# A stick-breaking attention trunk on one core: one transposed block in four split by ScalarE and GpSimd, and the running product's ones kept in a PSUM bank

## The chip, the core and the metric

The kernel runs on one core of a Trainium2 chip. A core has a matrix engine (TensorE, PE in the tables, with its weight loads as PEld), three engines that work element by element on 128 partitions (VectorE or DVE, ScalarE or ACT, GpSimd or POOL), a queue engine (SyncE, SP), a large on-chip memory (SBUF) and a small accumulator memory (PSUM) of 8 banks, each 128 x 512 float32. Each engine works through its own list of instructions in a fixed order, and waits on semaphores for what other engines and transfers have to deliver. The metric is the device time of one execution in microseconds (us); lower is better.

## The reference

A trunk of two layers on x of 2048 positions and 1024 channels, in float32. Layer 0 is a gated short convolution. Layer 1 is attention of 8 heads of width 64 without a softmax: a score z gives the weight exp(z + sum of log sigmoid(-z) over the keys from this one to the query), which is a difference of two neighbours of a running product of sigmoid(-z). The kernel therefore multiplies the running product itself with differences of neighbouring rows of v, and adds the first row.

```
z = jnp.einsum("bhqd,bhkd->bhqk", qb, kf[:, :, :kl]) * scale
mask = jnp.arange(kl)[None, :] < q_pos[:, None]
log_one_minus = jnp.where(mask, jax.nn.log_sigmoid(-z), 0.0)
rev = lax.cumsum(log_one_minus, axis=3, reverse=True)
weights = jnp.exp(jnp.where(mask, z + rev, -jnp.inf))
outs.append(jnp.einsum("bhqk,bhkd->bhqd", weights, vf[:, :, :kl]))
```

Around it stand RMS norms, one projection each for k and v and for q and the gate, `(o * silu(g)) @ w_out_b`, a residual and a last norm.

## The kernel before

The positions are reversed, so that the running product goes forward, and cut into four chunks of 512. Every float32 matmul is done as three matmuls in a reduced float format: an operand x is split in a high part (ScalarE copies it, with rounding) and a low part (x minus the high part, VectorE). That is `split` (L486), and its two instructions stand in the profile as CAST and TENSOR_TENSOR.

The attention (`attention`, L1050) goes over heads h, query chunks c and key chunks kc from c down to 0; one (c, h, kc) is a unit. Where kc equals c the unit is on the diagonal; 48 units of 80 lie off it (8 heads times 1 + 2 + 3). In a unit:

- for each of four query blocks qi: the scores z are two matmuls into a PSUM tile of tag "z" (L1073), of which there are NZ = 3; ScalarE takes sigmoid(-z/8) out of it into R in SBUF, which frees the bank; VectorE makes the running product of R in place (`tensor_tensor_scan`, L1083), with a column of `ones` (L390, in SBUF, read over and over) as its second operand and the last element of the key chunk before as its start; GpSimd copies R's last column to `cy`, the start of the next key chunk; on the diagonal GpSimd also fills above the diagonal (AFFINE_SELECT).
- for each of four key blocks kb from 3 down to 0: TensorE transposes the four R blocks into a PSUM tile `wt` (two of them), `split` (L1102) takes it out as `wth` and `wtl` in SBUF, and two matmuls with v add to `av`, the one PSUM tile of the head's output.

PSUM has its 8 banks given out in full: 2 for "lin" (projections), 3 for "z", 2 for "wt", 1 for "av". Banks of "z" also serve other stages (L615, L833, and the last products at L1202).

The order of the work is not written out. Every operation is recorded first; `places` gives each a place from PLAN, a table of two numbers for each part (an attention head of a chunk is "a" and two digits); and `order` runs a model of the engines in which the earliest operation that can start is taken, ties going by place, with costs from `cost` and buffers counted. `emit` (L351) then writes the instructions in that order, so nearly all have the line L353 in the profile, and each engine keeps its order whatever happens. In the model, VectorE and GpSimd take turns (`o.turns`, L220) where an instruction has two operands in SBUF and none in PSUM. The attention heads are mixed with projections (pk, pq, pv, pg), with the output projection of finished chunks (pob) and with the last norm of those (x2r). Transfers are issued from SyncE's and ScalarE's queues; those of k, v and q for the attention are ScalarE's.

Of the kernel before, what the change touches and what calls it, by code (L numbers as in the profile page):

```python
# [10 lines left out]
F32 = mybir.dt.float32  # L11
# [5 lines left out]
P = 128  # L17
# [4 lines left out]
CH = 512  # L22
# [3 lines left out]
Q, NPL = 4, 2  # L26
FIRST = (("act", [2, CH], NA), ("R", [CH], NR), ("q2", [2, CH], 2), ("kt", [CH], 2), ("vv", [CH], 2), ("wth", [CH], NWTS),
         ("wtl", [CH], NWTS), ("wraw", [Q, P], NRAW), ("whl", [2, Q, P], NWB))
NLIN, NZ, NWT, NAV = 2, 3, 2, 1

XNL = (0, 3, 6)
YLP = (2, 5)
# [329 lines left out]
def kernel(  # L362
# [15 lines left out]
    nc = Recorder(tc.nc)  # L378

    const = Pool(nc, "const", ctx.enter_context(tc.tile_pool(name="const", bufs=1)))  # L380
    psum = Pool(nc, "psum", ctx.enter_context(tc.tile_pool(name="psum", bufs=2, space=bass.MemoryType.PSUM)))
    dram = Pool(nc, "dram", ctx.enter_context(tc.tile_pool(name="dram", bufs=1, space=bass.MemoryType.DRAM)))
    sb = Pool(nc, "sb", ctx.enter_context(tc.tile_pool(name="sb", bufs=2)))
# [5 lines left out]
    make_identity(tc.nc, ident.real())  # L389
    ones = const.tile([P, P], F32, name="ones")  # L390
    nc.vector.memset(ones, 1.0)
    gains = {}

    def load_gain(name, src, eng=nc.gpsimd):
# [91 lines left out]
    def split(hi, lo, src, eng=nc.vector):  # L486
        nc.scalar.copy(hi, src)
        eng.tensor_sub(lo, src, hi.bitcast(F32))
# [561 lines left out]
    def attention(c, h, ot):  # L1050

        hb, hi_ = divmod(h, 2)
        nm0 = f"{c}_{h}"
        q2 = sb.tile([P, 2, CH], F32R, name=f"q2_{nm0}", tag="q2", bufs=2)
        for i in range(2):
            nc.scalar.dma_start(out=q2[i * 64:(i + 1) * 64, :, :].bitcast(F32), in_=q_d[c][hb][hi_ * 64:(hi_ + 1) * 64, :, :])
        av = psum.tile([P, CH], F32, name=f"av_{nm0}", tag="av", bufs=NAV)
        carry = [None] * 4
        for kc in range(c, -1, -1):
            nm = f"{nm0}_{kc}"  # L1060
            diag = kc == c
            own = (h + kc) % 2 == 0
            kt = sb.tile([P, CH], F32R, name=f"kt_{nm}", tag="kt" if own else "wraw", bufs=2 if own else NRAW)
            nc.scalar.dma_start(out=kt.bitcast(F32), in_=k_d[kc][h])
            vt = sb.tile([P, 4, 2, 64], F32R, name=f"vv_{nm}", tag="vv" if own else "wraw", bufs=2 if own else NRAW)
            nc.scalar.dma_start(out=vt.bitcast(F32), in_=v_d[kc][hb][:, hi_, :, :, :])
            ws = []
            if kc:
                cy = sb.tile([P, 4], F32, name=f"cy_{nm}", tag="cy", bufs=8)
            for qi in range(4):  # L1070
                lo = qi * P if diag else 0
                lom = min(lo, 256)
                ps = psum.tile([P, CH], F32, name=f"z_{nm}_{qi}", tag="z", bufs=NZ)  # L1073
                nc.tensor.matmul(ps[:, lom:CH], q2[:, 0, qi * P:(qi + 1) * P], kt[:, lom:CH], start=True, stop=False)
                nc.tensor.matmul(ps[:, lom:CH], q2[:, 1, qi * P:(qi + 1) * P], kt[:, lom:CH], start=False, stop=True)
                R = sb.tile([P, CH], F32, name=f"R_{nm}_{qi}", tag="R", bufs=NR)
                nc.scalar.activation(R[:, lo:CH], ps[:, lo:CH], AF.Sigmoid, scale=-0.125)
                if diag:

                    blk = R[:, lo:lo + P]  # L1080
                    nc.gpsimd.affine_select(out=blk, in_=blk, pattern=[[1, P]], base=0, channel_multiplier=-1,
                                            compare_op=ALU.is_gt, fill=1.0)
                nc.vector.tensor_tensor_scan(out=R[:, lo:CH], data0=R[:, lo:CH],  # L1083
                                             data1=ones[:, 0:1].to_broadcast([P, CH - lo]),
                                             initial=1.0 if diag else carry[qi], op0=ALU.mult, op1=ALU.mult)
                if kc:
                    nc.gpsimd.tensor_copy(cy[:, qi:qi + 1], R[:, CH - 1:CH])
                    carry[qi] = cy[:, qi:qi + 1]
                ws.append(R)
            for kb in range(3, -1, -1):  # L1090
                nq = kb + 1 if diag else 4
                n = max(256, nq * P)
                wt = psum.tile([P, CH], F32, name=f"wt_{nm}_{kb}", tag="wt", bufs=NWT)
                for qi in range(nq):
                    nc.tensor.transpose(wt[:, qi * P:(qi + 1) * P], ws[qi][:, kb * P:(kb + 1) * P], ident)
                first, final = diag and kb == 3, kc == 0 and kb == 0
                wh = sb.tile([P, CH], F32R, name=f"wth_{nm}_{kb}", tag="wth", bufs=NWTS)
                wl = sb.tile([P, CH], F32R, name=f"wtl_{nm}_{kb}", tag="wtl", bufs=NWTS)
                if nq == 1:
                    nc.gpsimd.memset(wh[:, P:2 * P].bitcast(F32), 0.0)  # L1100
                    nc.gpsimd.memset(wl[:, P:2 * P].bitcast(F32), 0.0)
                split(wh[:, 0:nq * P], wl[:, 0:nq * P], wt[:, 0:nq * P])  # L1102
                vs = vt[:, kb, :, :].rearrange("p a d -> p (a d)")
                nc.tensor.matmul(av[:, 0:n], vs, wh[:, 0:n], start=first, stop=False)
                nc.tensor.matmul(av[:, 0:n], vs, wl[:, 0:n], start=False, stop=final)
            if kc == 0:
                osl = slice(hi_ * 64, hi_ * 64 + 64)
                oth = slice(64 - hi_ * 64, 128 - hi_ * 64)
                nc.scalar.copy(ot[osl, :], av[oth, :])
                nc.vector.tensor_add(ot[osl, :], ot[osl, :], av[osl, :])  # L1110
# [154 lines left out]
    for c in range(NCH):  # L1265
        for hb in range(NH // 2):
            ot = sb.tile([P, CH], F32, name=f"ot_{c}_{hb}", tag="ot", bufs=2)
            for h in (2 * hb, 2 * hb + 1):
                part(f"a{c}{h}", attention, c, h, ot)
            if (c, hb) == (3, 3):  # L1270
                last_ot.append(ot)
            else:
                nc.sync.dma_start(out=og_d[c][hb], in_=ot)
# [37 lines left out]
```

## Time and profile before

| | |
|---|---|
| three executions | 1681.12, 1681.06, 1673.86 us, median 1681.06 |
| the profiled execution | 1683.09 us, its span 1680.9 us |
| share of the span in work: TensorE, VectorE, ScalarE, GpSimd | 97%, 80%, 47%, 31% |
| granted TensorE clock, mean | 0.992 |
| running products of 512 elements with a start from `cy` | 192, 1311 ns each |
| low parts of 512 elements from `wt` | 224, 680 ns each |

The span is what the profile shows from its first instruction to its last; 2.2 us of the profiled execution lie outside it. Times in a row of a group are the busy time of the whole group, then the mean of one instruction, then the engine's idle time just ahead of them and what ended it. A matmul's row is its latency, longer than the step to the next one, since matmuls are pipelined.

### The profile page before, as it was taken

Reading aid. Unit: us, or ns where it says so; the run is one execution under the profiler, and the core shown is the slowest. Engines: PE = TensorE matmul, PEld = TensorE weight load, DVE = VectorE, ACT = ScalarE, POOL = GpSimd, SP = SyncE. Lnnn points to the kernel's source line nnn. Section 1 sums busy time; section 2 is a strip of 40 time slices with the busy share of each in tenths; the row PEclk is TensorE's granted clock in tenths of the full one; section 3 lists DMA queues with packets and bytes.
Section 4 is the critical chain, followed back from the end, with each engine's and each line's share of the span. In section 5 each row is a group of like instructions: output and inputs, shape, how many; then the busy total and the mean of one; then the engine's idle time right before and its main releaser. Section 6 shows DMA issues by size and latency. Waiting matters only on the chain.

```text
span 1680.9 us, 23871 instructions
## 1 busy us (share of the span) xinstructions
PE 1623.6 (97%) x7828; PEld 1339.8 (80%) x7828; DVE 1345.1 (80%) x1944; ACT 787.7 (47%) x1483; POOL 524.6 (31%) x708
## 2 busy tenths in 40 slices
PE   6999999999999999998999999999999999999896
PEld 5878888888888887877778877887888888888775
DVE  6998788885436349798898788968999988999895
ACT  5444444432213125432544455645556656667452
POOL 5340000000000002357643142333333444556534
PEclk9999999999999999999999999999999999999997
DMA  9458889884473569999677899998756788779744
GB/s 275 163 182 307 296 303 306 278 304 145 147 213 97 192 208 314 365 353 345 213 240 248 288 368 299 357 278 244 222 182 184 229 261 283 247 237 282 228 158 140
DMA packets 226251, 419.48 MB, mean 250 GB/s; under 512 B 21072, under 2 KB 94800, under 8 KB 226128
## 3 DMA queue, kind: packets, MB, share of 16 engines
q1 hardware_dynamic: 194656, 358.15, 63.3%
q10 hardware_dynamic: 31312, 59.79, 12.4%
q8 instruction: 62, 1.02, 0.3%
q14 instruction: 61, 0.50, 0.1%
q0 software_dynamic: 160, 0.02, 0.0%
HBM read 265.06 MB, written 152.83 MB: 249 GB/s over the span
## 4 chain that ended last, share of the span: by engine, by line
PE 75%; DMA 7%; DVE 6%; issue 2%; ACT 2%; POOL 1%; SPq 0%; ACTq 0%; POOLq 0%; DVEq 0%
PE fa_B L353 9%; PE fa_C L353 9%; PE av L353 7%; PE z L353 6%; PE wt L353 6%; PE fd_B L353 5%; PE fd_C L353 4%; PE pob L353 4%; PE fa_o L353 3%; PE fe_C L353 2%; PE fe_B L353 2%; PE pg L353 2%; PE pq L353 2%; PE fa_kq L353 2%; PE pv L353 2%; PE pk L353 2%
## 5 line engine op out<-in xcount | busy, mean ns | idle before, releaser
L353 DVE TENSOR_TENSOR_SCAN R<-R,cy,ones 128x512 f32<-128x512 f32 x192 | 246.3, 1311 | 2.4 <-ACT R L353 2.1
L353 ACT CAST wth<-wt 128x512 fp32r<-128x512 f32 (+2 forms) x320 | 154.4, 526 | 178.9 <-PE wt L353 141.3
L353 DVE TENSOR_TENSOR wtl<-wt,wth 128x512 fp32r<-128x512 f32 (+2 forms) x320 | 180.6, 599 | 37.6 <-ACT wth L353 34.6
L353 PE MATMUL z<-kt,q 128*128 128x512 f32 (+2 forms) x640 | 179.1, 379 | 4.4 <-DMA q<-q_d 2.0
L353 ACT ACTIVATE R<-z 128x512 f32<-128x512 f32 (+2 forms) x320 | 158.9, 545 | 39.8 <-PE z L353 34.5
L353 PE MATMUL wt<-ident,R 128*128 128x128 f32 x1088 | 168.4, 273 | 0.1
L353 POOL COPY halo<-p 128x2 f32<-128x2 f32 x32 | 15.7, 490 | 482.2 <-DVE p L353 482.2
L353 PEld LDWEIGHTS wt<-ident,R 128*128 128x128 f32 x1088 | 133.4, 141 | 21.1 <-DVE R L353 0.7
L353 POOL COPY cy<-R 128x1 f32<-128x1 f32 x192 | 100.5, 526 | 135.8 <-DVE R L353 117.6
L353 PEld LDWEIGHTS z<-kt,q 128*128 128x128 f32 x640 | 111.4, 190 | 23.2 <-ACT R L353 4.5
L353 PE MATMUL av<-wth,vv 128*128 128x512 f32 (+1 forms) x320 | 119.5, 374 | 9.9 <-ACT wth L353 9.1
L353 PE MATMUL av<-wtl,vv 128*128 128x512 f32 (+1 forms) x320 | 122.7, 387 | 0.5 <-DVE wtl L353 0.4
L353 DVE TENSOR_TENSOR_SCAN R<-R,ones 128x256 f32<-128x256 f32 (+3 forms) x128 | 103.8, 838 | 8.8 <-POOL R L353 7.8
L353 POOL TENSOR_SCALAR_AFFINE_SELECT R<-R 128x128 f32<-128x128 f32 x128 | 68.1, 545 | 117.6 <-ACT R L353 116.4
L353 PE MATMUL pob<-og,whl_ob 128*128 128x512 f32 x360 | 102.8, 404 | 0.6 <-DVE x L353 0.4
L353 POOL TENSOR_TENSOR acc_x<-acc_x,sq_x 128x512 f32<-128x512 f32 x52 | 73.8, 1424 | 63.0 <-ACT sq_x L353 61.2
L353 PE MATMUL fa_C<-op_t,whl_s_C 128*128 128x512 f32 x336 | 85.2, 391 | 0.7 <-DVE op_t L353 0.7
L353 PE MATMUL fa_B<-op_t,whl_s_B 128*128 128x512 f32 x336 | 84.9, 390 | 0.0
L353 PEld LDWEIGHTS av<-wth,vv 128*128 128x128 f32 x320 | 60.4, 189 | 26.9 <-ACT wth L353 12.8
L353 PEld LDWEIGHTS fa_C<-op_t,whl_s_C 128*128 128x128 f32 x336 | 62.9, 188 | 14.7 <-DVE op_t L353 1.1
L353 PEld LDWEIGHTS pob<-og,whl_ob 128*128 128x128 f32 x360 | 64.6, 189 | 12.5 <-DVE x L353 0.8
L353 PEld LDWEIGHTS fa_B<-op_t,whl_s_B 128*128 128x128 f32 x336 | 63.0, 188 | 12.9
(581 smaller groups left out, 3779.4 us busy)
## 6 DMA issues: line engine op xcount, KB each, us to landing
kt<-k_d ACTq DMA_DIRECT2D x80, 256.0 KB, 4.6
vv<-v_d ACTq DMA_DIRECT2D x80, 256.0 KB, 4.7
q<-q_d ACTq DMA_DIRECT2D x64, 256.0 KB, 6.3
sw_s_C<-whl_s_C SPq DMA_DIRECT2D x24, 512.0 KB, 3.7
sw_s_B<-whl_s_B SPq DMA_DIRECT2D x24, 512.0 KB, 4.4
whl_s_C<-sw_s_C SPq DMA_DIRECT2D x24, 512.0 KB, 4.3
whl_s_B<-sw_s_B SPq DMA_DIRECT2D x24, 512.0 KB, 4.3
whl_ob<-sw_ob SPq DMA_DIRECT2D x24, 512.0 KB, 5.2
```

The costliest lines, as they stand in the source:

```text
L353: getattr(o.engine.engine, o.name)(*map(real, o.args), **{k: real(v) for k, v in o.kw.items()})
```

## The change

Two edits that go together. First, in the 48 units off the diagonal, the key block kb = 0 (the last of the four) is no longer split out of PSUM by ScalarE and VectorE. ScalarE copies `wt` to `wf`, a float32 tile in SBUF (tag "p", two buffers, which `out_v` and the convolution use too), ScalarE makes `wth` from `wf`, and GpSimd makes `wtl` as `wf` minus `wth`. Second, the ones of the running product lie in PSUM: a VectorE memset fills one column of a bank of its own, `one`, and the scores' tiles go from three to two to make room. PLAN and all other numbers stay.

```diff
-NLIN, NZ, NWT, NAV = 2, 3, 2, 1
+OFF = (0,)
+NLIN, NZ, NWT, NAV = 2, 2, 2, 1
...
     nc.vector.memset(ones, 1.0)
+    one = psum.tile([P, CH], F32, name="one", tag="one", bufs=1)[:, 0:1]
+    nc.vector.memset(one, 1.0)
...
                 nc.vector.tensor_tensor_scan(out=R[:, lo:CH], data0=R[:, lo:CH],
-                                             data1=ones[:, 0:1].to_broadcast([P, CH - lo]),
+                                             data1=one.to_broadcast([P, CH - lo]),
                                              initial=1.0 if diag else carry[qi], op0=ALU.mult, op1=ALU.mult)
...
-                split(wh[:, 0:nq * P], wl[:, 0:nq * P], wt[:, 0:nq * P])
+                if diag or kb not in OFF:
+                    split(wh[:, 0:nq * P], wl[:, 0:nq * P], wt[:, 0:nq * P])
+                else:
+                    wf = sb.tile([P, CH + 2], F32, name=f"wf_{nm}_{kb}", tag="p", bufs=2)
+                    nc.scalar.copy(wf[:, 0:CH], wt)
+                    split(wh, wl, wf[:, 0:CH], nc.gpsimd)
```

The model sees other costs, so the order moves as well. The heads follow one another as before on TensorE, and most rows keep their neighbours; three places show what differs. A name such as z_6_0_2 is head, key chunk and query block; wth_6_0_1 is head, key chunk and key block; the last number of a name only counts tiles.

First, TensorE near the end, the scores of the last key chunk of the last head (chunk 3, head 6). Before, and then after:

```order
L353 MATMUL z_6_0_0_17089<-kt_6_0_16660,q_3_6_16270 128x512 [waits DMAHW7_49]
L353 MATMUL z_6_0_0_17089<-kt_6_0_16660,q_3_6_16270 128x512
L353 MATMUL z_6_0_1_17095<-kt_6_0_16660,q_3_6_16270 128x512
L353 MATMUL av_6_17015<-wth_6_2_3_17086,vv_6_2_16706 128x512 [waits DMAHW1_49,Activation_49]
L353 MATMUL z_6_0_1_17095<-kt_6_0_16660,q_3_6_16270 128x512
L353 MATMUL z_6_0_2_17104<-kt_6_0_16660,q_3_6_16270 128x512 x2
L353 MATMUL z_6_0_3_17109<-kt_6_0_16660,q_3_6_16270 128x512 [waits Activation_49]
L353 MATMUL z_6_0_3_17109<-kt_6_0_16660,q_3_6_16270 128x512
```

```order
L354 MATMUL z_6_0_0_17157<-kt_6_0_16767,q_3_6_16371 128x512 [waits DMAHW7_49,Activation_49]
L354 MATMUL z_6_0_0_17157<-kt_6_0_16767,q_3_6_16371 128x512
L354 MATMUL z_6_0_1_17163<-kt_6_0_16767,q_3_6_16371 128x512 [waits Activation_49]
L354 MATMUL av_6_17123<-wth_6_3_1_17159,vv_6_3_16817 128x256 [waits Activation_49]
L354 MATMUL z_6_0_1_17163<-kt_6_0_16767,q_3_6_16371 128x512
L354 MATMUL z_6_0_2_17173<-kt_6_0_16767,q_3_6_16371 128x512 [waits Activation_49]
L354 MATMUL z_6_0_2_17173<-kt_6_0_16767,q_3_6_16371 128x512
L354 MATMUL z_6_0_3_17179<-kt_6_0_16767,q_3_6_16371 128x512 [waits Activation_49]
L354 MATMUL z_6_0_3_17179<-kt_6_0_16767,q_3_6_16371 128x512
```

With three tiles only the fourth tile's first matmul waits for ScalarE; with two, each tile does, and less stands between the last matmul of one tile and the first of the next in the same bank: between z_6_0_0 and z_6_0_2 two matmuls of z_6_0_1 and one of 256 columns, between z_6_0_1 and z_6_0_3 the two of z_6_0_2.

Second, GpSimd's list near the end, ahead of the last low part (x2r is the last norm of chunk 2, cy the carried column). Before, and then after:

```order
L353 COPY cy_6_1_17098<-R_6_1_3_17049 128x1 [waits DVE_49]
L353 TENSOR_TENSOR x2r_7_17164<-x2r_7_17164,pbs_15994 128x512 [waits DMAHW4_49,Pool_49]
L353 TENSOR_TENSOR x2r_0_16823<-x2r_0_16823,pbs_17251 128x512 [waits DMAHW0_49,Activation_49]
L353 TENSOR_TENSOR x2r_1_16840<-x2r_1_16840,pbs_17251 128x512 [waits DMAHW2_49]
L353 TENSOR_TENSOR x2r_2_16877<-x2r_2_16877,pbs_17251 128x512
L353 TENSOR_TENSOR x2r_3_17177<-x2r_3_17177,pbs_17251 128x512 [waits DMAHW5_49,DVE_49]
L353 TENSOR_TENSOR x2r_4_17256<-x2r_4_17256,pbs_17251 128x512 [waits DMAHW3_49,DMAHW0_49,Pool_49]
```

```order
L354 TENSOR_TENSOR wtl_6_1_0_17333<-wf_6_1_0_17321,wth_6_1_0_17324 128x512 [waits PE_49,Activation_49]
L354 TENSOR_TENSOR x2r_0_16903<-x2r_0_16903,pbs_17335 128x512 [waits DMAHW7_49,Activation_49]
L354 TENSOR_TENSOR x2r_1_16930<-x2r_1_16930,pbs_17335 128x512 [waits DMAHW1_49,DMAHW0_49]
L354 TENSOR_TENSOR x2r_2_16952<-x2r_2_16952,pbs_17335 128x512 [waits DMAHW6_49]
L354 TENSOR_TENSOR x2r_3_17248<-x2r_3_17248,pbs_17335 128x512 [waits DMAHW5_49]
L354 TENSOR_TENSOR x2r_4_17338<-x2r_4_17338,pbs_17335 128x512 [waits DMAHW3_49,DMAHW0_49,Pool_49]
L354 TENSOR_TENSOR wtl_6_0_0_17420<-wf_6_0_0_17398,wth_6_0_0_17407 128x512 [waits PE_49,Activation_49]
L354 TENSOR_TENSOR x2r_5_17415<-x2r_5_17415,pbs_17335 128x512 [waits DMAHW6_49,DMAHW4_49,Pool_49]
```

The low part of the last block, wtl_6_0_0, which was VectorE's, now stands on GpSimd behind five products x2r_0 to x2r_4.

Third, ScalarE's list at the same block, with the last copies of the head behind it. Before, and then after:

```order
L353 CAST wth_6_0_2_17274<-wt_6_0_2_17258 128x512 [waits DVE_49,PE_49]
L353 CAST wth_6_0_1_17303<-wt_6_0_1_17294 128x512 [waits DVE_49,PE_49]
L353 CAST wth_6_0_0_17310<-wt_6_0_0_17299 128x512 [waits DVE_49,PE_49]
L353 COPY ot_3_16226<-av_6_17015 64x512 [waits PE_49]
L353 CAST og_3_17361<-ot_3_16226 128x512 [waits DVE_49]
```

```order
L354 CAST wth_6_0_2_17363<-wt_6_0_2_17347 128x512 [waits PE_49,Pool_49]
L354 CAST wth_6_0_1_17391<-wt_6_0_1_17381 128x512 [waits DVE_49,PE_49]
L354 COPY wf_6_0_0_17398<-wt_6_0_0_17387 128x512 [waits PE_49]
L354 CAST wth_6_0_0_17407<-wf_6_0_0_17398 128x512 [waits DVE_49,Activation_49]
L354 COPY ot_3_16312<-av_6_17123 64x512 [waits PE_49]
L354 CAST og_3_17478<-ot_3_16312 128x512 [waits DVE_49]
```

One copy out of PSUM (wf) has come in between the high parts of blocks 1 and 0, and the high part of block 0 now reads wf, not the PSUM tile.

## The prediction

> **What bounds the kernel now.** I read the page's first part, then the windows of the stages that the change touches, then what TensorE waited for in them.
>
> ```profile
> PE 1623.6 (97%) x7828; PEld 1339.8 (80%) x7828; DVE 1345.1 (80%) x1944; ACT 787.7 (47%) x1483; POOL 524.6 (31%) x708
> ...
> 924.00:1176.00 252.00, 243.22 (x1255) 200.32 (x1253) 205.90 (x291) 132.52 (x278) 79.21 (x159) 0.99 0.94 306
> 1176.00:1554.00 378.00, 377.20 (x2079) 318.60 (x2078) 352.99 (x473) 237.99 (x480) 172.88 (x272) 1.00 0.75 236
> 1554.00:1600.00 46.00, 40.76 (x211) 33.73 (x210) 37.92 (x46) 21.51 (x45) 25.24 (x36) 0.93 0.75 221
> 1600.00:1640.00 40.00, 38.76 (x214) 31.57 (x213) 39.42 (x61) 20.92 (x41) 12.54 (x23) 1.00 0.50 160
> ```
>
> The columns of a window are its length, then the busy time of TensorE, its weight loads, VectorE, ScalarE and GpSimd, each with its count of instructions, then the granted clock. The attention begins at about 960 us. In its long middle (1176 to 1554) TensorE is idle for 0.8 us of 378, while VectorE works 93% of the time: VectorE is nearly full, but nobody waits for it. A busy TensorE is not yet one at its pace, so I look at the pace too:
>
> ```profile
> 378.00:420.00 42.00, 42.00 (x187) 34.75 (x186) 24.47 (x36) 11.73 (x20) 1.06 (x4) 1.00 0.46 145
> 1545.99 1.03 PE L353 MATMUL wt<-ident,R 128*128 128x128 f32 x8
> ```
>
> Far ahead of the attention, with nothing to wait for, 187 matmuls of 512 columns fill 42 us: 0.225 us each. Eight transposes take 1.03 us, of which the last one's latency is 0.27 (its group: 273 ns): 0.109 us each. What TensorE lost in the attention is this:
>
> ```profile
> PE av L353 <- ACT wth L353: 9.1, 8, 5.2
> PE z L353 <- DMA q<-q_d: 2.0, 1, 2.0
> PE z L353 <- ACT R L353: 2.0, 3, 1.3
> PE av L353 <- PE pq L353: 0.8, 1, 0.8
> PE av L353 <- DVE wtl L353: 0.4, 2, 0.2
> ...
> 1566.12 0.80 PE L353 MATMUL av<-wth,vv 128*128 128x512 f32 x1 [5.21 <-ACT wth L353]
> 1566.72 3.19 PE L353 MATMUL pg<-xn,whl_gg 128*128 128x512 f32 x7
> ...
> 1565.07 0.32 ACTq L353 DMA_DIRECT2D kt<-k_d  x1
> 1565.49 1.07 ACT L353 CAST wth<-wt 128x512 fp32r<-128x512 f32 x2 [6.36 <-DMA x2r<-x_d]
> ```
>
> (TensorE's waits from 924 to 1640: total, times, longest; then the one long wait.) Of 9.1 us for `wth`, 5.2 are one event in which ScalarE stood behind a transfer of its own queue; the matmuls after it run at half pace for a while (seven in 3.19 us, where the clock of the window is 0.93). VectorE's low parts cost TensorE 0.4 us. So the bound is TensorE's own list, and the four windows hold 8.8 + 0.8 + 5.2 + 1.2 = 16.0 us of idle TensorE, most of it behind ScalarE and transfers.
>
> **The change part by part.** The rows that carry the sizes (whole span, forms apart; then two rows with least, median and longest ns; then a stretch in order of time):
>
> ```profile
> L353 DVE TENSOR_TENSOR_SCAN R<-R,cy,ones 128x512 f32<-128x512 f32 x192 | 246.3, 1311 | 2.4 <-ACT R L353 2.1
> L353 DVE TENSOR_TENSOR wtl<-wt,wth 128x512 fp32r<-128x512 f32 x224 | 145.0, 680 | 30.6 <-ACT wth L353 29.9
> L353 PE MATMUL z<-kt,q 128*128 128x512 f32 x448 | 143.4, 407 | 4.4 <-DMA q<-q_d 2.0 <-ACT R L353 2.0 <-DMA kt<-k_d 0.3
> L353 ACT ACTIVATE R<-z 128x512 f32<-128x512 f32 x224 | 127.7, 609 | 32.8 <-PE z L353 28.1 <-PE wt L353 2.5 <-POOL R L353 0.4
> L353 ACT CAST wth<-wt 128x512 fp32r<-128x512 f32 x224 | 122.6, 591 | 139.5 <-PE wt L353 115.2 <-DVE R L353 6.7 <-DMA x2r<-x_d 6.4
> L353 POOL COPY cy<-R 128x1 f32<-128x1 f32 x192 | 100.5, 526 | 135.8 <-DVE R L353 117.6 <-DVE yr_x L353 7.4 <-DVE t_x L353 4.0
> L353 DVE TENSOR_TENSOR fr_a_B<-fr_a_B,fr_a_B 128x512 f32<-128x512 f32 x32 | 22.1, 690 | 0.9
> L353 ACT CAST whl_s_C<-fr_a_C 128x512 fp32r<-128x512 f32 x32 | 19.8, 621 | 25.1 <-DVE fr_a_C L353 13.7 <-PE fd_B L353 6.3 <-PE fa_C L353 2.0
> ...
> L353 DVE TENSOR_TENSOR_SCAN R<-R,cy,ones x192: 1249/1272/2322, 998.3 to 1640.3; 128x512 f32<-128x512 f32 x192
> L353 POOL COPY cy<-R x192: 173/232/1877, 991.3 to 1632.5; 128x1 f32<-128x1 f32 x192
> ...
> 1199.08 2.45 DVE L353 TENSOR_TENSOR_SCAN R<-R,cy,ones 128x512 f32<-128x512 f32 x2
> 1200.42 1.09 POOL L353 COPY cy<-R 128x1 f32<-128x1 f32 x1 [1.40 <-DVE R L353]
> 1201.47 1.30 POOL L353 TENSOR_TENSOR ogr<-ogr,sga 128x512 f32<-128x512 f32 x1
> 1202.71 0.18 POOL L353 COPY cy<-R 128x1 f32<-128x1 f32 x1
> ```
>
> *VectorE* loses 48 low parts of 680 ns, 32.6 us. With the ones out of SBUF it should also stop blocking GpSimd: the copy of one column takes 1.09 us while a running product runs (to 1201.53) and 0.18 us beside the low parts, which read PSUM. [...] On the path this is worth at most the 16.0 us of idle TensorE and at least nothing; TensorE waited 0.4 us for VectorE directly and a few times for `wth` queued behind late work, so I take -2.
>
> Whether the running product is slower with an operand in PSUM no row shows. The nearest are the VectorE rows above, 680 ns from PSUM and 690 with both in SBUF: between nothing and a gain of 10 ns, and I take nothing. [...]
>
> *ScalarE* gets 48 copies more of 591 ns, 28 us, and the 48 high parts come from SBUF (621 instead of 591 ns, 1.4 us in all). It was busy 238 of 378 us in the middle; cover is there, but ScalarE is what z and `wth` wait for, and this enters the next term.
>
> *The scores' third bank.* TensorE may start tile i+2 only when ScalarE has read tile i; before, i+3. Along TensorE's list I counted, for each of the 320 tiles, the matmuls between the last of one tile and the first of the next in its bank, at 0.225 us (0.172 and 0.117 for 384 and 256 columns, in proportion, 0.109 for a transpose). The median distance falls from 3.34 to 1.79 us; in the last head's place in the order it is 0.57 and 0.45. What is needed: 407 ns of the last matmul and 609 ns of ScalarE, less the 0.225 already counted, and 0.16 for two handoffs (0.08 each, from ScalarE's end at 1641.24 to GpSimd's start at 1641.32 in the rows of the tail, below): 0.95 us with ScalarE free, the lower bound; 1.25 with half of another ScalarE instruction ahead, the upper. Summing what each distance lacks:
>
> - at 0.95: 1.0 us before, 7.0 after: +6
> - at 1.1: 2.5 before (the trace has 2.0 of z waiting for ScalarE, so this fits best), 11.3 after: +9
> - at 1.25: 5.8 before, 21.0 after: +15
>
> TensorE has no slack to give these back, and each wait is in its own list: I take +9.
>
> *The low part on GpSimd.* Chain from the last transposes: 0.27, ScalarE 0.59 and 0.62, GpSimd 1.30, four handoffs of 0.08, less the transpose's 0.11: 3.0 us. TensorE's list leaves 3.5 us at the median over the 48 (a tenth under 3.0, least 2.0). So it fits, until GpSimd is late: in 10 of the 48, a 512-wide product stands directly in front on its list (x2r, ogr, an accumulation, or the low part before). At 1.3 us each, less 0.5 of slack, that is up to 8; at least it is nothing. I take +3, nearer to the low end, as GpSimd is busy for only 173 of 378 us in the middle, so that most such products will have ended by then. Behind a late low part, `cy` and the diagonal fills wait on GpSimd, and `av` on TensorE. GpSimd pays 48 x 1.3 = 62 us, and the copies, at 0.18 instead of 0.53, give back up to 67.
>
> *The tail.*
>
> ```profile
> 1640.66 0.58 ACT L353 COPY pbs<-prb_x 128x512 f32<-128x512 f32 x1 [2.55 <-PE prb_x L353]
> 1641.32 6.29 POOL L353 TENSOR_TENSOR x2r<-x2r,pbs 128x512 f32<-128x512 f32 x5 [5.98 <-ACT pbs L353]
> ...
> 1647.74 0.39 PE L353 MATMUL av<-wtl,vv 128*128 128x512 f32 x1
> 1647.96 6.06 PE L353 MATMUL pob<-og,whl_ob 128*128 128x512 f32 x26
> 1653.86 2.43 PE L353 MATMUL pol<-og,whl_obl 128*128 128x512 f32 x10
> ...
> 1652.62 0.68 DVE L353 TENSOR_TENSOR og<-ot,og 128x512 fp32r<-128x512 f32 x1
> ```
>
> The five x2r products end at 1647.6, and the last low part would follow at 1648.9, some 1.2 us after the place where its matmul stands now. The chain from there to the last products (og ready at 1653.3, pol at 1653.86) has 0.5 us to spare, and its cover of pob shrinks from 26 matmuls to 24. I take +1 (0 to +1.5).
>
> Sum: -2 + 9 + 3 + 1 = +11 on the profiled execution's 1683.1 (1680.9 of span and 2.2 around it), 1694. That execution lies 2.0 over the median of the runs, so on that scale: **1692**.
>
> **The rivals.** *Faster.* VectorE at 93 to 99% sets the pace of the attention after all, and relief lets all engines keep to the list, the long wait at 1560 included: all 16.0 us of idle TensorE gone and no wait for z, 1665. For it: the nearly full VectorE, running products of 1311 ns that GpSimd stretches. Against: 0.4 us of waits for VectorE. *No change.* The shortfalls of z overlap with other waits (a TensorE that waits for z finds `wth` ready), or the relief equals them: 1681. For it: a wait that is moved costs nothing twice. *GpSimd decides.* If the low part is late by more than its 0.5 us of slack in those 10 places, and z needs 1.25 us since ScalarE is fuller: +15 + 8 + 1.5 = 24.5, 1706. *The ones in PSUM don't free GpSimd*: `cy` stays at 0.53 us, GpSimd has 62 us more than now, and this comes out at the same 1706.
>
> **How the numbers follow.** Forecast 1692 (its own range, from the terms' bounds, 1687 to 1700): 0.38. No change: 0.29. Faster: 0.20. GpSimd decides, ones included: 0.13. A measurement here can tell 0.5%, 8.4 us, so 1689.5 is the bound to slower; of the forecast's 0.38 I count 0.06 below it. Faster 0.20, same 0.29 + 0.06 = 0.35, slower 0.32 + 0.13 = 0.45. The range goes from 1670, which leaves out the full gain only, to 1707.
>
> **What would show it.** Running products near their median of 1.27 us in the mean too, and `cy` near 0.2 us in the mean: GpSimd is free of them. TensorE's wait for R from ScalarE at z going from 2.0 to about 11 us: the bank term. Waits of `av` for `wtl` from GpSimd of some us, next to x2r: the GpSimd term. Wrong if TensorE's idle time in the attention falls, or if a single wait of over 5 us behind a transfer comes or goes: such a one moves the time by as much as any term here and hangs on the new order alone.

## The result and the profile after

| | before | after |
|---|---|---|
| median | 1679.93 us (13 runs, 1672.88 to 1685.65) | 1686.46 us (13 runs, 1680.57 to 1691.91) |
| ratio | | 1.0045, 95% interval 1.0029 to 1.0062 |
| profiled execution, its span | 1683.09, 1680.9 us | 1688.69, 1686.9 us |

The change costs 7.5 us by the ratio (6.5 by the medians); with 13 runs on each side the interval of the ratio leaves 1 out. The page of after, first part, and its windows over the same stretches as before (columns as there; the last two rows are two further windows, the tail and a piece of it):

```profile
PE 1630.8 (97%) x7828; PEld 1339.0 (79%) x7828; DVE 1309.0 (78%) x1897; ACT 818.6 (49%) x1531; POOL 482.2 (29%) x756
```

```profile
924.00:1176.00 252.00, 244.26 (x1256) 201.86 (x1255) 197.72 (x286) 137.56 (x286) 64.50 (x165) 0.99 0.93 307
1176.00:1554.00 378.00, 374.72 (x2046) 312.10 (x2045) 322.94 (x431) 252.17 (x500) 141.16 (x297) 1.00 0.72 230
1554.00:1600.00 46.00, 46.00 (x253) 38.25 (x252) 42.63 (x53) 30.29 (x60) 24.79 (x47) 1.00 0.86 277
1600.00:1640.00 40.00, 38.19 (x205) 29.81 (x205) 35.88 (x53) 23.24 (x45) 13.84 (x26) 1.00 0.50 156
...
1640.00:1687.00 47.00, 29.94 (x132) 24.56 (x132) 24.94 (x46) 12.45 (x21) 20.18 (x16) 0.77 0.36 121
1660.00:1664.00 4.00, 4.00 (x15) 3.24 (x14) 3.19 (x6) 2.35 (x4) 1.07 (x1) 0.78 0.00 0
```

VectorE lost 36 us of work and GpSimd, although it took over 48 products, 42. In the four attention windows TensorE now idles 7.7 + 3.3 + 0.0 + 1.8 = 12.8 us, less than the 16.0 before. So the kernel got slower while TensorE idled less in the stages that the change touches. The counts of matmuls in the windows say more: in the long middle TensorE starts 33 fewer (2046 for 2079), and from 1554 to 1600, where before had its one long wait, 42 more (253 for 211). At the middle's mean step of 0.18 us (378 us for 2079) that is an estimated 6.0 us lost and 7.6 won back. What TensorE waited for from 924 to 1646, and the groups and single durations of the changed instructions:

```profile
PE z L354 <- ACT R L354: 4.4, 6, 1.6
PE av L354 <- ACT wth L354: 4.4, 4, 2.5
PE av L354 <- DVE wtl L354: 2.0, 4, 1.0
```

```profile
L354 DVE TENSOR_TENSOR_SCAN R<-R,cy,one 128x512 f32<-128x512 f32 x192 | 238.6, 1266 | 5.8 <-ACT R L354 5.3 <-issue 0.2
L354 POOL TENSOR_TENSOR wtl<-wf,wth 128x512 fp32r<-128x512 f32 x48 | 62.1, 1294 | 85.9 <-ACT wth L354 57.5 <-issue 8.6 <-PE prb_x L354 5.2
```

```profile
L354 POOL COPY cy<-R x192: 173/183/650, 1006.8 to 1633.9; 128x1 f32<-128x1 f32 x192
L354 DVE TENSOR_TENSOR_SCAN R<-R,cy,one x192: 1244/1270/1281, 1008.7 to 1640.8; 128x512 f32<-128x512 f32 x192
```

The ones in PSUM do what they are meant to. The longest running product falls from 2322 to 1281 ns, the longest carried copy from 1877 to 650, and their means from 1311 to 1266 and from 526 to 195. No wait of a matmul is put down to a low part of GpSimd, and one of a weight load is (0.5 us). The bank term shows as 4.4 us of z waiting for ScalarE, where it was 2.0; and the one wait of 5.2 us behind a transfer, with the half-pace stretch after it (seven matmuls in 3.19 us), did not come again.

I split the span at the last eight transposes of the last head. TensorE's list from there, in order of time, after:

```profile
1645.08 1.04 PE L354 MATMUL wt<-ident,R 128*128 128x128 f32 x8
...
1648.04 2.21 PE L354 MATMUL pob<-og,whl_ob 128*128 128x512 f32 x9
1650.08 0.39 PE L354 MATMUL av<-wtl,vv 128*128 128x512 f32 x1
1650.31 5.60 PE L354 MATMUL pob<-og,whl_ob 128*128 128x512 f32 x24
1657.98 7.33 PE L354 MATMUL pol<-og,whl_obl 128*128 128x512 f32 x24 [2.07 <-ACT og L354]
```

and the same piece before:

```profile
1644.80 1.03 PE L353 MATMUL wt<-ident,R 128*128 128x128 f32 x8
...
1653.86 5.60 PE L353 MATMUL pol<-og,whl_obl 128*128 128x512 f32 x24
```

Up to these transposes the two executions differ by 0.3 us (1644.80 and 1645.08); from there to the end of the span it is 36.1 us before and 41.8 after. Of the 6.0 us by which the two spans differ, 5.7 stand behind the transposes:

- the last low product of `av` stands 5.00 us behind the transposes (1645.08 to 1650.08), 2.94 before (1644.80 to 1647.74), with 15 `pob` matmuls between them instead of 6: +2.1;
- from it to the first `pol` it takes 7.90 us instead of 6.12; two `pob` fewer stand there (24 for 26), but TensorE waits 2.07 us for `og`: +1.8;
- the 24 `pol` matmuls take 7.33 us instead of 5.60, at a granted clock of 0.78 in the window from 1660: +1.7.

Not all of this is lost in the tail. Seven `pob` matmuls more stand behind the transposes (39 for 32), and at 0.225 us each they are 1.6 us of work that the kernel before had done earlier. What remains to the tail itself is the wait for `og` and the slow `pol`, 3.8 us.

The wait for `og` comes from VectorE. Its list after, from the last additions of the output to `og`, and then ScalarE's high part of `og`, for which the first `pol` waits:

```profile
1651.12 0.68 DVE L354 TENSOR_TENSOR ot<-ot,av 64x512 f32<-64x512 f32 x1 [0.83 <-ACT ot L354]
1651.87 0.69 DVE L354 TENSOR_TENSOR x<-x,pob 128x512 f32<-128x512 f32 x1
1652.47 0.65 DVE L354 SCALAR_TENSOR_TENSOR ot<-ot,v_first,sgl 128x128 f32<-128x128 f32 x1
1653.91 0.69 DVE L354 TENSOR_TENSOR x<-x,pob 128x512 f32<-128x512 f32 x1 [0.79 <-PE pob L354]
1654.52 1.22 DVE L354 SCALAR_TENSOR_TENSOR ot<-ot,v_first,sgl 128x128 f32<-128x128 f32 x1
1655.95 0.69 DVE L354 TENSOR_TENSOR x<-x,pob 128x512 f32<-128x512 f32 x1 [0.21 <-PE pob L354]
1656.56 0.72 DVE L354 SCALAR_TENSOR_TENSOR ot<-ot,v_first,sgl 128x128 f32<-128x128 f32 x2
1657.96 0.69 DVE L354 TENSOR_TENSOR og<-ot,og 128x512 fp32r<-128x512 f32 x1 [0.68 <-ACT og L354]
...
1657.31 0.62 ACT L354 CAST og<-ot 128x512 fp32r<-128x512 f32 x1 [6.22 <-DVE ot L354]
```

and before:

```profile
1648.78 0.68 DVE L353 TENSOR_TENSOR ot<-ot,av 64x512 f32<-64x512 f32 x1 [0.84 <-ACT ot L353]
1649.49 0.61 DVE L353 SCALAR_TENSOR_TENSOR ot<-ot,v_first,sgl 128x128 f32<-128x128 f32 x2
1650.03 0.68 DVE L353 TENSOR_TENSOR x<-x,pob 128x512 f32<-128x512 f32 x1
1650.62 0.61 DVE L353 SCALAR_TENSOR_TENSOR ot<-ot,v_first,sgl 128x128 f32<-128x128 f32 x2
...
1651.27 0.62 ACT L353 CAST og<-ot 128x512 fp32r<-128x512 f32 x1 [2.52 <-DVE ot L353]
```

The four block products of `ot` had one addition `x<-x,pob` between them; now one stands ahead of them and two between them, and these two wait for a group of `pob` matmuls to end (0.79 and 0.21 us). Their work is the same, their places in the list are not. From the last product of `av` to the high part of `og` it takes 7.85 us (1650.08 to 1657.93) instead of 4.15 (1647.74 to 1651.89).

### The profile page after: what moved, and what is told of

It reads as the page before. It is cut to its first block, busy times and chain, and to the rows that moved or that the text cites. A ratio compares the mean times of both kernels' runs of the same rounds, so it can differ in the third digit from the quotient of the medians.

```text
span 1686.9 us, 23939 instructions
## 1 busy us (share of the span) xinstructions
PE 1630.8 (97%) x7828; PEld 1339.0 (79%) x7828; DVE 1309.0 (78%) x1897; ACT 818.6 (49%) x1531; POOL 482.2 (29%) x756
## 4 chain that ended last, share of the span: by engine, by line
PE 73%; DMA 9%; DVE 7%; issue 2%; ACT 1%; POOL 1%; ACTq 0%; SPq 0%; POOLq 0%; DVEq 0%
PE fa_B L354 9%; PE fa_C L354 9%; PE av L354 7%; PE z L354 6%; PE wt L354 6%; PE pob L354 5%; PE fd_B L354 4%; PE fd_C L354 4%; PE pv L354 2%; PE pg L354 2%; PE fe_C L354 2%; PE fa_kq L354 2%; PE fe_B L354 2%; PE fa_vg L354 2%; PE pk L354 2%
## 5 line engine op out<-in xcount | busy, mean ns | idle before, releaser
L354 DVE TENSOR_TENSOR_SCAN R<-R,cy,one 128x512 f32<-128x512 f32 x192 | 238.6, 1266 | 5.8 <-ACT R L354 5.3
L354 PE MATMUL z<-kt,q 128*128 128x512 f32 (+2 forms) x640 | 194.4, 388 | 5.1 <-ACT R L354 4.4
L354 ACT CAST wth<-wt 128x512 fp32r<-128x512 f32 (+3 forms) x272 | 134.8, 514 | 127.3 <-PE wt L354 100.1
L354 ACT ACTIVATE R<-z 128x512 f32<-128x512 f32 (+2 forms) x320 | 165.5, 541 | 54.2 <-PE z L354 46.4
L354 DVE TENSOR_TENSOR wtl<-wt,wth 128x512 fp32r<-128x512 f32 (+3 forms) x272 | 153.8, 585 | 47.0 <-ACT wth L354 40.2
L354 PE MATMUL wt<-ident,R 128*128 128x128 f32 x1088 | 173.3, 272 | 0.0
L354 DVE TENSOR_TENSOR_SCAN R<-R,one 128x256 f32<-128x256 f32 (+3 forms) x128 | 98.9, 804 | 15.0 <-POOL R L354 14.9
L354 POOL TENSOR_TENSOR wtl<-wf,wth 128x512 fp32r<-128x512 f32 x48 | 62.1, 1294 | 85.9 <-ACT wth L354 57.5
L354 PEld LDWEIGHTS av<-wtl,vv 128*128 128x128 f32 x320 | 60.4, 189 | 15.4 <-DVE wtl L354 4.5
```

The lines of the kernel that those rows point to most:

```text
L354: getattr(o.engine.engine, o.name)(*map(real, o.args), **{k: real(v) for k, v in o.kw.items()})
```

## The experiments

Twelve kernels, in three sets; each set has its own runs of the kernel before on the same chip (medians 1679.09, 1680.40, 1679.44 us), and a ratio compares a kernel with those runs (it is not the quotient of the two medians, and differs from that by up to 1.1 per mille). The full change ran in none of these sets, so a comparison with it goes over its own ratio of 1.0045. A per mille is 1.7 us. The theories: B, the scores' third bank costs what was forecast; T, the loss is in the tail; P, freeing GpSimd's copies is worth time; G, the low parts come late on GpSimd; O, the loss is in the order that the model finds for other costs, and not in any of the instructions.

**One part at a time.** First the bank alone:

```diff
-NLIN, NZ, NWT, NAV = 2, 3, 2, 1
+NLIN, NZ, NWT, NAV = 2, 2, 2, 1
```

> The kernel before with two score tiles in place of three and nothing else; the ones stay in SBUF, every split on VectorE, and one PSUM bank lies idle. Theory B (the bank, as in the prediction): the waits of TensorE for ScalarE at z go from 2.0 us to about 11, and the time is +9 us, a ratio near 1.005. Theory T (the tail, read off the profile of the changed kernel: from the last eight transposes to the end it has 41.8 us where the kernel before has 36.1, and the last low part sits on GpSimd): nothing of the loss is here, a ratio within 0.002 of 1.

Measured: 1683.86 us, ratio 1.0028 (1.0012 to 1.0045), so 4.7 us, between the two forecasts. TensorE waited 3.6 us at z for ScalarE (the row is shown below, with g1), not 11: B's cost is not there, and T's "nothing" is not either.

The full change with its ones back in SBUF and three banks:

```diff
-NLIN, NZ, NWT, NAV = 2, 2, 2, 1
+NLIN, NZ, NWT, NAV = 2, 3, 2, 1
...
-    one = psum.tile([P, CH], F32, name="one", tag="one", bufs=1)[:, 0:1]
-    nc.vector.memset(one, 1.0)
+    one = ones[:, 0:1]
```

> The 48 blocks split by ScalarE and GpSimd, but three score tiles and the ones in SBUF. Theory B: without the bank term only the low part's lateness (+3), the tail (+1) and the relief (-2) are left, ratio 1.001. Theory T: the whole loss is here, +6 us, ratio near 1.0035. If the ones in SBUF matter, running products get longer than 1311 ns in the mean and the copies cy stay near 0.5 us, since GpSimd now has 48 wide products more that read SBUF; the ratio is then above that of the full change.

Measured: 1716.44 us, ratio 1.0219 (1.0198 to 1.0239), 37 us more than before and far over both theories. What the expectation said for the case that the ones in SBUF matter is what came: longer running products, and a ratio above that of the full change. Its groups, and one of TensorE's waits:

```profile
L354 DVE TENSOR_TENSOR_SCAN R<-R,cy,ones 128x512 f32<-128x512 f32 x192 | 257.6, 1363 | 6.9 <-ACT R L354 5.1 <-POOL wth L354 1.3 <-issue 0.2
L354 POOL TENSOR_TENSOR wtl<-wf,wth 128x512 fp32r<-128x512 f32 x48 | 77.8, 1620 | 79.5 <-ACT wth L354 56.5 <-issue 13.9 <-POOL cy L354 3.4
```

```profile
PE av L354 <- POOL wtl L354: 3.6, 5, 1.9
```

A low part on GpSimd takes 1620 ns in place of 1294, a running product 1363 in place of 1266, and now TensorE does wait for GpSimd. Of the 48 low parts (1460 ns at the median), 25 take over 1.4 us, and each of these overlaps a running product in the trace. So the two edits do go together: the split without the ones in PSUM is the worst of all. (This kernel has an order of its own as well, so the 37 us are not the price of the overlaps alone; the loss is three times what another order cost the kernel before in c1, below.)

The ones in PSUM and two banks, no block moved:

```diff
-OFF = (0,)
+OFF = ()
```

> The ones in PSUM and two score tiles, but every split on VectorE as before. Theory B: the bank's +9 less the relief of the running products (1311 to 1266 ns, 192 of them, 8.6 us of VectorE, of which about 1 counts): ratio 1.004 to 1.005. Theory T: no GpSimd in the tail, so the ratio is within 0.002 of 1. The copies cy near 0.2 us in both.

Measured: 1680.91 us, ratio 1.0009 (0.9998 to 1.0020). That is T's range and not B's. Against e1 the ones give back some 3 us (1.9 per mille, with about 2.0 of uncertainty, from the two intervals).

The full change, but the last head of the last chunk keeps the old split, in its three units off the diagonal:

```diff
-                if diag or kb not in OFF:
+                if diag or kb not in OFF or (c, h) == (NCH - 1, 6):
```

> The changed kernel, but the last head of the last chunk (chunk 3, head 6) keeps its three blocks on VectorE; 45 of 48 stay with ScalarE and GpSimd. Theory B: it gains the tail's +1 only, ratio 1.003 to 1.004. Theory T: from the last transposes to the end the time goes back from 41.8 to about 36 us, and the ratio to between 0.999 and 1.001.

Measured: 1682.74 us, ratio 1.0021 (1.0007 to 1.0035), between the two forecasts and 4 us less than the full change (2.4 per mille, with 2.2 of uncertainty). Its `pol` begin at 1655.33 without a wait, and take 5.60 us. From the first of its last eight transposes to the end it takes 37.6 us, not 36. So far this points at the tail. But each of these kernels was also ordered anew, and what that is worth was open.

**What the order alone does.** The kernel before and the full change, both with another cost of a semaphore in the model. The instructions are the same; only their order differs:

```diff
-SEM = 0.11
+SEM = 0.12
```

> Control: the kernel before, with the model's cost of a semaphore 0.12 instead of 0.11 us. The instructions are the same, only the order that the model finds differs. Theory B (the bank and the tail are real costs of the change): this says how far the order alone moves the time; ratio 0.998 to 1.002. Rival O (the 4.5 per mille of the change are luck of the order): the ratio differs from 1 by 3 per mille or more, in either direction.

> Control: the full change with the same cost of a semaphore, 0.12. Theory B: still slower than the control without the change by 3 to 6 per mille, 1684 to 1690 us; the wait of the last products for og or something like it remains in the tail. Rival O: no steady distance to the control, less than 2 per mille or with the other sign.

Measured: 1691.42 us for the kernel before, ratio 1.0071 (1.0050 to 1.0092), and 1690.46 us for the full change, 1.0058 (1.0039 to 1.0077). The old kernel in another order loses 12 us, more than by the whole change, as rival O asked; and in these orders the change makes no difference that can be told (1.3 per mille faster, with 2.8 of uncertainty). Where c1 lost it, TensorE in order of time:

```profile
1018.47 0.79 PE L353 MATMUL z<-kt,q 128*128 128x512 f32 x1 [3.45 <-DMA kt<-k_d]
...
1653.75 1.03 PE L353 MATMUL wt<-ident,R 128*128 128x128 f32 x8
...
1664.16 5.60 PE L353 MATMUL pol<-og,whl_obl 128*128 128x512 f32 x24
```

In the two profiles all of it stands before the last transposes (1653.75, 9.0 us later than before), a wait of 3.45 us behind a transfer among it; its tail is 35.5 us long, near before's 36.1. The tail of c2 is like that of after: 2.31 us of waiting for `og` ahead of `pol`, which come at 1658.03.

**Other ways to free GpSimd.** If the copies of the carried column are what the ones in PSUM free, they can also be put elsewhere, with no bank given up. On VectorE, in the kernel before:

```diff
-                    nc.gpsimd.tensor_copy(cy[:, qi:qi + 1], R[:, CH - 1:CH])
+                    nc.vector.tensor_copy(cy[:, qi:qi + 1], R[:, CH - 1:CH])
```

> The kernel before with the 192 copies of the carried column on VectorE instead of GpSimd; three score banks, ones in SBUF, no split moved. Theory P (the 3 us that ones in PSUM gave back came from GpSimd's copies no longer standing against running products): the same relief without the price of the bank, running products 1.27 us in the mean, ratio 0.997 to 0.999. Rival N (that relief was worth something only where two banks made waits): VectorE has some 15 us of copies more and nobody waited for it; ratio 0.999 to 1.002.

And with no copy at all, the next running product starting from the column itself:

```diff
-                    nc.gpsimd.tensor_copy(cy[:, qi:qi + 1], R[:, CH - 1:CH])
-                    carry[qi] = cy[:, qi:qi + 1]
+                    carry[qi] = R[:, CH - 1:CH]
```

> The kernel before without any copy of the carried column: the running product starts from the last column of the R tile of the key chunk before, so that tile is held longer. Theory P: running products 1.27 us in the mean, GpSimd 100 us less busy, ratio 0.997 to 0.999. Rival N: nobody waited for these copies, 0.999 to 1.001. Rival H (the 13 tiles of R held longer become the limit): waits of ScalarE for a free R appear and z waits more, ratio above 1.002.

Measured: 1696.42 us, ratio 1.0102 (1.0077 to 1.0128), and 1687.85 us, 1.0045 (1.0027 to 1.0062). f2 takes work away (GpSimd 441.5 us in place of 524.6) and loses 7.5 us. Both ratios lie over the ranges of P and N. But the relief that P counts on did not come: the running products take 1327 ns (f1) and 1350 ns (f2) in the mean, where 1.27 us was asked for and the kernel before has 1311. (The copies that N put at some 15 us of VectorE took 23.4 in f1, 138 ns each.) So these two kernels do not say what the relief is worth. H has the ratio that it asked for in f2, but not its waits: among the eleven longest totals of ScalarE's waits from 924 to 1646 (5.0 us and more) none is for a free R, and z waited only 1.5 us for ScalarE. Of the running products of f2, the shortest, the median and the longest:

```profile
L353 DVE TENSOR_TENSOR_SCAN R<-R,R,ones x192: 1249/1270/2327, 999.4 to 1643.6; 128x512 f32<-128x512 f32 x192
```

The long ones are still there without any copy. In the traces each running product over 1.4 us (28 in f2, 13 in the kernel before, diagonal ones included) overlaps a wide product of GpSimd of over 1 us; in after, with the ones in PSUM, there is none over 1.4 us. Whether f1 and f2 lose by their edits or by their orders was not taken apart.

**The order held fixed.** The last four keep a kernel's order on every engine and change one thing when the instructions are written. The order of e1, but its tiles get three banks:

```diff
-            self.tile = self.pool.real.tile(self.shape, self.dtype, **self.kw)
+            kw = dict(self.kw, bufs=3) if self.kw.get("tag") == "z" else self.kw
+            self.tile = self.pool.real.tile(self.shape, self.dtype, **kw)
```

> The order of the kernel with two score banks (e1), word for word on every engine, but the tiles are given three banks: only the waits for a bank go. Theory B (the waits for a bank cost time): 2 to 4 us less than e1, as e1 waited 3.6 us of z for ScalarE; ratio 1.000 to 1.0015. Theory O (what e1 lost comes from the order that the model found): ratio as e1's, 1.002 to 1.004.

Measured: 1681.75 us, ratio 1.0019 (1.0006 to 1.0032). TensorE's waits from 924 to 1646, e1 and then g1:

```profile
PE z L353 <- ACT R L353: 3.6, 8, 0.8
PE av L353 <- ACT wth L353: 3.5, 6, 1.1
PE av L353 <- DVE wtl L353: 2.0, 2, 1.0
```

```profile
PE av L354 <- ACT wth L354: 6.7, 9, 1.8
PE av L354 <- DVE wtl L354: 3.4, 6, 1.0
...
PE z L354 <- ACT R L354: 1.0, 3, 0.5
```

The third bank takes 2.6 us of waits away at z, and 4.6 come up at `av`: TensorE, earlier at one place, waits at the next. On the time it is 0.9 per mille, 1.5 us, with about 2.1 per mille of uncertainty: between the two forecasts, and not told from nothing. And with three banks again, e1's order alone is still 1.9 per mille slower than before.

The order of e1, two banks, the running products reading their ones from PSUM:

```diff
+            if o.name == "tensor_tensor_scan":
+                kw["data1"] = real(self.one.to_broadcast([P, o.kw["out"].extent()[1]]))
```

> The order of e1 on every engine, two banks, but the running products read their ones from a PSUM bank. Theory P (freeing GpSimd's copies gives time on the path): some 3 us less than e1, ratio 1.000 to 1.0015, carried copies at 0.19 us. Theory O (that gain was of the order): the copies fall to 0.19 us and the time stays, ratio 1.002 to 1.004.

Measured: 1681.49 us, ratio 1.0018 (1.0005 to 1.0031), copies of 191 ns in the mean, running products of 1265: 1.0 per mille, 1.7 us, under e1, between the two forecasts and not to be told from nothing.

The order of the full change, the 48 low parts written to VectorE:

```diff
+            if engine.name == POOL and o.name == "tensor_sub" and o.args[0].base.kw["name"].startswith("wtl_"):
+                engine = self.vector
```

> The order of the full change, but the 48 low parts run on VectorE (wf and the ones in PSUM stay); they now have two inputs in SBUF at some 0.69 us. Theory G (low parts on GpSimd come late): 4 to 6 us less than the full change, ratio 1.001 to 1.002. Theory O: as the full change, 1.004 to 1.005; VectorE has 33 us more and nobody waits.

Measured: 1692.16 us, ratio 1.0085 (1.0067 to 1.0104), 4.0 per mille *over* the full change, with 2.5 of uncertainty. Neither forecast had that. Theory G falls: in this order, which was made for GpSimd, the low parts are better there, at 1294 ns, than on VectorE. The loss stands ahead of the last transposes, which come 5.6 us later than in after:

```profile
L357 DVE TENSOR_TENSOR wtl<-wf,wth 128x512 fp32r<-128x512 f32 x48 | 33.3, 695 | 4.0 <-ACT wth L357 3.7
```

The same, but only the one last low part, behind the five x2r products:

```diff
+            if engine.name == POOL and o.name == "tensor_sub" and o.args[0].base.kw["name"].startswith("wtl_3_6_0_0"):
+                engine = self.vector
```

> The order of the full change, but the one last low part, behind the five x2r products, runs on VectorE. Theory T (the tail): its matmul comes 1 to 2 us earlier, og is ready earlier, the wait of 2.07 us for og and the half clock behind it go, 2 to 5 us less than the full change, ratio 1.0015 to 1.0035. Theory O (the gain of e4 came from another order): less than 1 us, ratio 1.004 to 1.005.

Measured: 1687.36 us, ratio 1.0058 (1.0042 to 1.0074): nothing gained. Its tail, VectorE and TensorE in order of time:

```profile
1643.45 1.04 PE L357 MATMUL wt<-ident,R 128*128 128x128 f32 x8
...
1645.91 1.12 DVE L357 TENSOR_TENSOR wtl<-wf,wth 128x512 fp32r<-128x512 f32 x1
...
1648.45 0.39 PE L357 MATMUL av<-wtl,vv 128*128 128x512 f32 x1
...
1652.28 0.69 DVE L357 TENSOR_TENSOR x<-x,pob 128x512 f32<-128x512 f32 x1 [1.09 <-PE pob L357]
...
1654.32 0.69 DVE L357 TENSOR_TENSOR x<-x,pob 128x512 f32<-128x512 f32 x1 [0.58 <-PE pob L357]
...
1656.23 5.73 PE L357 MATMUL pol<-og,whl_obl 128*128 128x512 f32 x24 [1.95 <-ACT og L357]
```

The low part is ready at 1647.03, 1.4 us before its matmul; that stands 5.00 us behind the transposes as it did in after, and `pol` come 7.78 us behind it (7.90 in after). The low part no longer sets either. The matmul has its place behind nine `pob` matmuls on TensorE's list, and `og` comes behind the two additions on VectorE's list that wait for `pob` (the rows at 1652.28 and 1654.32). The model chose these places when it had the last low part end late.

The tails of all the kernels, from the first of their last eight transposes:

| kernel | transposes at | `pob` matmuls from there to `pol` | wait of `pol` for `og` | from the transposes to the end |
|---|---|---|---|---|
| before | 1644.80 | 32 | none | 36.1 |
| e1, two banks | 1645.85 | 32 | none | 36.4 |
| g1, g2, in the order of e1 | 1645.76, 1647.08 | 32, 32 | none | 35.4, 34.8 |
| e3, no block moved | 1641.29 | 40 | none | 38.7 |
| e4, last head on VectorE | 1643.96 | 40 | none | 37.6 |
| c1, before in another order | 1653.75 | 38 | none | 35.5 |
| f1, f2 | 1655.05, 1648.11 | 31, 32 | none | 35.8, 36.5 |
| after | 1645.08 | 39 | 2.07 | 41.8 |
| g3, g4, in the order of after | 1650.64, 1643.45 | 39, 39 | 1.96, 1.95 | 39.4, 40.7 |
| c2, after in another order | 1644.67 | 39 | 2.31 | 41.2 |
| e2, split only | 1674.35 | 26 | 3.50 | 39.2 |

The first `pol` of three of the last rows (e2, c2, g3):

```profile
1685.70 7.38 PE L354 MATMUL pol<-og,whl_obl 128*128 128x512 f32 x24 [3.50 <-ACT og L354]
...
1658.03 5.73 PE L354 MATMUL pol<-og,whl_obl 128*128 128x512 f32 x24 [2.31 <-ACT og L354]
...
1663.39 7.39 PE L357 MATMUL pol<-og,whl_obl 128*128 128x512 f32 x24 [1.96 <-ACT og L357]
```

Where the last unit's low part was ordered for GpSimd, the first `pol` waits 1.95 to 3.50 us for `og`; in no other kernel does it wait. The tails there take 39.2 to 41.8 us, the others 34.8 to 38.7. The length of the tail says less than the wait: it also holds how many `pob` matmuls an order leaves for it, and behind `pol` come another 19.2 (g3) to 22.2 us (g4) that differ whatever stands ahead. No version was faster than the kernel before.

## Why the prediction was right, and where it was not

Its 1692 us, with 1670 to 1707 around it, was 5.5 us over the median of 1686.46, and the side was right. It was no nearer than the rival *No change*: 1681 lies 5.5 us under the median. The median also lies under the prediction's own bound to slower, 1689.5; to that side it gave 0.35, to slower 0.45. The sum came this near by a wrong division, and by its own tests ("z going from 2.0 to about 11 us", "waits of av for wtl from GpSimd of some us") the forecast's mechanism did not come about. In the two profiles an estimated 6.0 us are lost in the middle, 7.6 are won back where the long wait went, 3.8 are lost in the tail, and the rest in smaller pieces; that their total of 6.0 comes anywhere near the forecast +11 is luck. And the terms' bounds as given add up to 1671 to 1706, not to the 1687 to 1700 that the prediction calls its own range.

- *The ones free GpSimd.* Right. Means of 1.27 and near 0.2 us were asked for, and 1266 and 195 ns came. The rival that they don't is out.
- *VectorE's relief, -2.* Not contradicted, and not shown: g2 against e1 gives -1.7 us, not told from zero. (One reading was off: the carried copy of 0.18 us stands beside a split of q, 1202.63 to 1203.31, and not beside the low parts, which end at 1202.71; that split reads PSUM too.) The step that an operand in PSUM costs the running product nothing held: medians of 1272 ns before and 1270 after.
- *The scores' third bank, +9.* This is the term that was mis-sized. The shortfalls were counted one by one on TensorE's list and added, as if "TensorE has no slack to give these back". In the trace z waited 4.4 us, not 11. In g1 the third bank takes 2.6 us of such waits away, the waits at `av` grow by 4.6, and the time changes by 1.5 us, not told from nothing. The rival *No change* had this mechanism in words ("a TensorE that waits for z finds wth ready").
- *The low part on GpSimd, +3.* No matmul's wait is put down to it, and g3 speaks against the sign: in the same order the low parts cost less there than on VectorE. That 33 us of VectorE work, put back, cost 6.7 us (with 4.2 of uncertainty) suggests that a nearly full VectorE (89% busy from 1176 to 1554 in g3, 85% in after) is worth more than its 0.4 us of direct waits; that the order was made for GpSimd may be another reason.
- *The tail, +1.* Too small: 3.8 us in the profile without the `pob` work that only moved, about 4 by e4 (with 3.6 of uncertainty). The working set 1.2 us of lateness against 0.5 of slack and took the rest of the chain as it stood before. The slack was larger than that: `pol` starts with the high part of `og`, which before is ready at 1651.89, 2.0 us ahead of it. What failed is the rest of the chain. The working read the second place of the quoted order for what stands ahead of the low part on GpSimd, and not TensorE's and VectorE's lists behind it, where its matmul had gone 2.1 us back and two more additions had come ahead of and between the products of `ot`: 7.85 us from `av` to `og` in place of 4.15, more than the slack holds.
- *A wait over 5 us behind a transfer.* The prediction named it as what would make it wrong. The wait of 5.2 us and the reduced clock after it went (granted 0.93 from 1554 to 1600 before, 1.00 after). In the two profiles this paid for what the middle lost (42 matmuls more from 1554 to 1600, 33 fewer before). Taken from the steps between matmuls, against the prediction's paces for each width, the middle (1176 to 1554) lost an estimated 5.7 us more than before, short waits included that no row shows as idle: 1.9 ahead of z, 2.5 ahead of `av`, 0.9 ahead of the transposes. So the third bank's +9 is not hidden there either.
- *What the prediction lacked* is the price of a new order as such. It let the order in by single waits only. c1 shows that the old kernel loses 12 us when the model's cost of a semaphore changes by 0.01 us. An edit that changes costs draws another order for the whole program, and its luck comes into the same 7.5 us. So these can't be called the price of the change's instructions: between c1 and c2 that price is nothing that can be told. What is shown of the change's own is the wait for `og` in the tail, 1.95 to 3.50 us, in every kernel whose order had the last low part on GpSimd and in no other.

How much of the rest of the loss is order and how much the edits stays open; one pair of other orders (c1 and c2) does not settle an average over orders.

## What to carry to other kernels

Where a planner sets the order, an edit is measured against a spread of orders, not against one: change a cost that means nothing, and see how far the time moves, before a few per mille are put down to an edit. To take the price of one resource, keep the order and change only the resource, as g1 to g4 did. And a late instruction has two prices, its own lateness and the places that the lists behind it then have; the second stays when the first is mended.

## What the runs showed of the hardware

- With its one-column operand in SBUF, a running product and a GpSimd instruction that overlapped took longer in a part of the cases, on both sides. In the kernel before, 50 of the 224 running products of 512 elements overlap a GpSimd product of over 1 us: 1466 ns in the mean, 2322 at most, 13 of them over 1.4 us; the other 174 take 1260 in the mean and 1322 at most. With that column in PSUM, in after, 83 overlap one: 1262 in the mean, 1281 at most; the other 141 take 1256 and 1280. GpSimd's one-column copies took 780 ns in the mean before where they overlapped a running product (108) and 201 where not (84), in after 184 (97) and 206 (95). GpSimd's low parts took 1620 ns in the mean and 2290 at most in e2, where after has 1294 and 1420. What it costs in time is not taken apart from the order: e2, with 48 wide products more and the column in SBUF, lost 37 us.
- The 24 `pol` ran slow after some of the short waits for `og`, and not after others: 7.33 us after a wait of 2.07 us (after, granted clock 0.80 from 1656 to 1660 and 0.78 from 1660 to 1664), 7.39 after 1.96 (g3) and 7.38 after 3.50 (e2), but 5.73 after 2.31 (c2) and after 1.95 (g4, granted clock 1.00 over both stretches). The length of the wait alone does not decide it.
